# Gate blocks of the RG-LRU packed by halves of the rows, with high weights from a rounding DMA of GpSimd

## The chip, the cores and the metric

The kernel runs on one core of one Trainium2 chip. The metric is the time of one execution on the device, in microseconds, the median of several executions. One execution of each kernel is also recorded by the hardware profiler, and all views below are of that execution. The engines are named as in the profile: PE (TensorE, the matmuls; PEld are its weight loads), DVE (VectorE), ACT (ScalarE), POOL (GpSimd) and SP (SyncE, which here only issues transfers). A row of the profile such as `L127` names a line of the kernel file, which may be that of a helper.

## The reference

One decoder layer on a sequence of 512 tokens with 2048 channels, in float32. What matters here is the recurrent branch: a causal convolution of width 4, two gates by block-diagonal matrices (16 blocks of 64 channels), and a linear recurrence.

```python
h = rms_norm(x) * (1.0 + scale) + shift          # scale, shift, gate from silu(c) @ w_ada + b_ada
proj = h @ w_in                                  # xr, gr, qc, kvc, kr, ga
...
xc = causal_depthwise_conv(xr, conv_w) + conv_b
xb = xc.reshape(B, S, RNN_BLOCKS, RNN_BLOCK)     # 16 blocks of 64 channels
r = sigmoid(einsum('bshi,hij->bshj', xb, w_rg_a).reshape(B, S, C) + b_rg_a)
i = sigmoid(einsum('bshi,hij->bshj', xb, w_rg_x).reshape(B, S, C) + b_rg_x)
log_a = -LRU_C * r * softplus(-lru_lambda)
a = exp(log_a)
b = sqrt(-expm1(2.0 * log_a)) * (i * xc)
y_rnn = linear_recurrence(a, b) * silu(gr)
y_att = mla_branch(qc, kvc, kr, ...) * silu(ga)
x = x + gate * (concat(y_rnn, y_att) @ w_out)
```

## The kernel before

Everything is kept transposed: channels on the 128 rows of SBUF, the 512 tokens along a row. A float32 product is made of three matmuls in the chip's rounded float32 (`fp32r`): each operand is split into a high part, its rounded value, and a low part, the rest. `mm3` and `mm3s` issue high × high, high × low and low × high, with the weights as the stationary operand. The split of a weight tile is done by `wsplit` (L205): ACT copies the raw tile with rounding (`whi<-wraw`), and DVE subtracts (`wlo<-wraw,whi`). `wload` (L200) first issues the transfer of the raw tile on SP. The pools of these tiles hold 3 raw, 2 high and 2 low tiles (`WIDE`).

The program goes through these stages. Up to about 214 us of the profiled execution the modulation, the normalised input h and most of the input projection are computed: the input channels of w_in are taken in 16 groups of 128, and the first 9 of them are done here for all column blocks. Then comes the loop over `MORDER[:24]` (L812), to about 330 us: for each of 24 blocks of 128 output columns, `proj_last` (L528) loads a 448 KB tile (7 groups of input channels, 128 x 896 elements), issues 14 matmuls with the high weights and 7 with the low, and adds the sum to what is stored. I call one turn of this loop a step. Between the steps stand the parts of the recurrent branch for blocks of 128 channels, m = 0 to 7: `rg_conv` (L688, convolution and gates), `rg_decay`, `rg_scan` (the recurrence, one DVE instruction) and `fin_gr` (L803, product with silu(gr), and its split into yh and yl), and the latent parts of the attention (`latent`, `do_kr`). The attention stage and the output projection follow, to the end; there, generators in a list `pipe` are advanced in turn, and the remaining 8 blocks of projection and the output projection are issued as fillers between the attention's pieces.

In `rg_conv`, two blocks of 64 channels share the 128 rows. The matrix of a gate is therefore a 128 x 128 tile with two 64 x 64 blocks on its diagonal and zeros elsewhere; a tile of 128 x 256 holds both gates. The convolved input xc is split into xh and xl (ACT and DVE, 128 rows each), the weights into gh and gl, and three matmuls into bank `pr` and three into bank `pi` follow. ACT then applies the two sigmoids with their biases:

```python
mm3(pr, gh[:, 0:P], gl[:, 0:P], xh, xl, True, True)
mm3(pi, gh[:, P:2 * P], gl[:, P:2 * P], xh, xl, True, True)
tab(x, pr, AF.Sigmoid, bias=vec[:, C_BA + m:C_BA + m + 1])
tab(ig, pi, AF.Sigmoid, bias=vec[:, C_BX + m:C_BX + m + 1])
```

Two calls stand behind each of steps 4, 5, 9 and 10; `rg_decay` behind 6 and 11, the square roots behind 7 and 12. Behind steps 19 and 23 `fin_gr` is called for four blocks each.

What sets the order: each engine executes its own instructions in the order in which the program holds them, and waits there for the results that it needs. SP's order is that of the code (it is scheduled by hand). The order on PE, DVE, ACT and POOL is laid out by a list scheduler when the program is built, from its own estimates of durations; `issue_after` and the chaining of table functions in `tab` bind some instructions behind others. So an instruction that is moved or shortened in the code can change the order of its neighbours.

Of the kernel before, what the change touches and what calls it, by code (L numbers as in the profile page):

```python
# [12 lines left out]
F32 = mybir.dt.float32  # L13
F32R = mybir.dt.float32r
BF16 = mybir.dt.bfloat16
I32 = mybir.dt.int32
AF = mybir.ActivationFunctionType
ALU = mybir.AluOpType
AX = mybir.AxisListType

P = 128
S = 512
# [23 lines left out]
WARM = (7, 10)  # L46
NACC = 6
GRATE = 1.1
BANKS = dict(u=(0, 1, 3), f=(2,), sc=(4, 5), tp=(6,), op=(6,), tq=(7,), oa=(2, 3, 0, 1, 7, 4, 5, 6))
QUOTA = (13, 6, 5, 6, 10)  # L50
MAGIC = 12582912.0

C_BADA, C_CW, C_CB, C_BA, C_BX, C_LAM, C_QA, C_KVA, NVEC = 0, 48, 80, 88, 96, 104, 112, 116, 120
R_QN, R_KN, R_QR, R_KR, R_IF, R_ID, R_MK, NROW = 0, 128, 256, 320, 384, 416, 544, 672

TWO_PI = 2.0 * math.pi
# [30 lines left out]
def body(ctx, nc, tc, a):  # L87
    V, G, A, PE, DMA = nc.vector, nc.gpsimd, nc.scalar, nc.tensor, nc.sync
    last_tab = [None]

    def act(out, in_, func, **kw):
        return A.activation(out=out, in_=in_, func=func, **kw)  # L92

    def tab(out, in_, func, **kw):
        if last_tab[0] is None:
            i = act(out, in_, func, **kw)
        else:
            with tc.issue_after(last_tab[0]):
                i = act(out, in_, func, **kw)
        last_tab[0] = i.ins if hasattr(i, "ins") else i  # L100
        return i
# [9 lines left out]
    def ins_of(i):  # L111
        return i.ins if hasattr(i, "ins") else i
# [6 lines left out]
    def tt(o, x, y, op):  # L119
        return V.tensor_tensor(out=o, in0=x, in1=y, op=op)  # L120

    def split(hi, lo, src):
        act(hi, src, AF.Copy)
        return tt(lo, src, hi.bitcast(F32), ALU.subtract)
# [73 lines left out]
    wlast = [None]  # L198

    def wload(src, n, after=None):  # L200
        raw = wraw()
        DMA.dma_start(out=raw[:, :n], in_=src)
        return wsplit(raw, n, after)

    def wsplit(raw, n, after=None, hi_after=None):  # L205
        hi, lo = wtile("whi", "whi"), wtile("wlo", "wlo")
        with tc.issue_after(hi_after) if hi_after is not None else nullcontext():
            act(hi[:, :n], raw[:, :n], AF.Copy)
        with tc.issue_after(after) if after is not None else nullcontext():
            wlast[0] = ins_of(tt(lo[:, :n], raw[:, :n], hi[:, :n].bitcast(F32), ALU.subtract))  # L210
        return hi, lo

    NB = 18
    vec = cst.tile([P, NVEC], F32, name="vec")
    row = cst.tile([P, NROW], F32, name="row")
# [312 lines left out]
    def proj_last(n, kind, parts):  # L528
        ps = bank(kind, "pp")
        m = MORDER[n]  # L530
        for k0, k1 in parts:
            wh, wl = wload(a["win3"][n, :, k0 * P:k1 * P], (k1 - k0) * P)
            mm3s(ps, wh, wl, hs(KM + k0, KM + k1), k0 == 0, KM + k1 == NK)
            if KM + k1 == NK:
                if n < N1:
                    stt(slot[m], ps, b0[:, n:n + 1], slot[m], ALU.add, ALU.add)
                else:
                    tt(slot[m], ps, slot[m], ALU.add)
            yield
# [145 lines left out]
    def tmp(name):  # L685
        return rg.tile([P, S], F32, tag="t", name=name, bufs=4)

    def rg_conv(m):  # L688
        w = lambda t: vec[:, C_CW + 8 * t + m:C_CW + 8 * t + m + 1]
        x = slot[XR + m]  # L690
        xc = half(XC, xcn, xcc, "xc")
        act(xc, x, AF.Identity, scale=w(3), bias=vec[:, C_CB + m:C_CB + m + 1])
        for s in (1, 2, 3):
            stt(xc[:, s:S], x[:, 0:S - s], w(3 - s), xc[:, s:S], ALU.mult, ALU.add)
        xs = rg.tile([P, 2, S], F32R, tag="xs", name="xs", bufs=2)
        xh, xl = xs[:, 0], xs[:, 1]
        split(xh, xl, xc)
        raw = rg.tile([P, 256], F32, tag="graw", name="graw", bufs=2)
        DMA.dma_start(out=raw, in_=a["wrg"][m])
        gh = rg.tile([P, 256], F32R, tag="gh", name="gh", bufs=2)  # L700
        gl = rg.tile([P, 256], F32R, tag="gl", name="gl", bufs=2)
        split(gh, gl, raw)
        pr = bank("aux", "pr")
        mm3(pr, gh[:, 0:P], gl[:, 0:P], xh, xl, True, True)
        pi = bank("aux", "pi")
        mm3(pi, gh[:, P:2 * P], gl[:, P:2 * P], xh, xl, True, True)
        tab(x, pr, AF.Sigmoid, bias=vec[:, C_BA + m:C_BA + m + 1])
        ig = tmp("ig")
        tab(ig, pi, AF.Sigmoid, bias=vec[:, C_BX + m:C_BX + m + 1])
        tt(xc, ig, xc, ALU.mult)  # L710
        return xc

# [87 lines left out]

    yh, yl = {}, {}

    def fin_gr(m):  # L803
        yt = tmp("yt")
        tt(yt, slot[XR + m], slot[GR + m], ALU.mult)
        yh[m] = pjt(XR + m, F32R, f"yh{m}")
        yl[m] = pjt(GR + m, F32R, f"yl{m}")
        split(yh[m], yl[m], yt)

    banks(mm=(0, 1, 2, 3), aux=(4, 5, 6, 7))  # L810
    xcs, als = {}, {}
    for n, m in enumerate(MORDER[:24]):  # L812
        run(proj_last(n, "mm", ((0, 7),)))
        if n == 16:
            proj_kr(2)
            do_kr()
        if n in (19, 23):
            for m in range(n - 19, n - 15):
                tab(slot[GR + m], slot[GR + m], AF.Silu)
            for m in range(n - 19, n - 15):  # L820
                fin_gr(m)
        if n in (4, 5):
            for t in (2 * n - 8, 2 * n - 7):
                xcs[t] = rg_conv(t)
        if n == 6:
            for t in range(4):
                als[t] = rg_decay(t)
        if n in (7, 12):
            for t in range(4):
                t += 4 * (n > 7)  # L830
                tab(slot[XR + t], slot[XR + t], AF.Sqrt)
        for n0, t0 in ((7, 0), (15, 4)):
            if n0 <= n < n0 + 4:
                t = t0 + n - n0
                with tc.issue_after(wlast[0]):
                    rg_scan(t, xcs[t], als[t])
        if n in (9, 10):
            for t in (2 * n - 14, 2 * n - 13):
                xcs[t] = rg_conv(t)
        if n == 11:  # L840
            for t in range(4, 8):
                als[t] = rg_decay(t)
        if KVC <= m < KVC + 4:
            latent(m, KVC, 0, kvh, kvl, C_KVA)
        if QC <= m < QC + 4:
            latent(m, QC, 1, qh, ql, C_QA)
# [5 lines left out]
    p3ctx = ExitStack()  # L852
    p3 = p3ctx.enter_context(tc.tile_pool(name="p3", bufs=1))
    mask = p3.tile([P, S], F32, name="mask")
    V.memset(mask[:, :S - P], 0.0)
    act(mask[:, S - P:], row[:, R_MK:], AF.Copy)
    HT = FREE[5:]
    banks(**BANKS)
    KT, QT = HT[0:3], HT[3:6]
# [256 lines left out]
    def paced():  # L1116
        st = 0
        for n, _ in enumerate(fillers()):
            if n >= GSTART:
                gates(int(st * GRATE))  # L1120
                st += 1
            if n in XSTEPS:
                oload()
            yield
# [97 lines left out]
    wh, wl = wload(a["wlast"], 4 * P)  # L1222
# [21 lines left out]
def _layout(x, c, positions, w_ada, b_ada, w_in, conv_w, conv_b, w_rg_a, b_rg_a, w_rg_x, b_rg_x, lru_lambda,  # L1244
            q_a_norm, w_uq, kv_a_norm, w_ukv, q_norm_nope, q_norm_rope, k_norm_nope, k_norm_rope, w_out):
    f = np.float32
# [9 lines left out]
    cols = np.concatenate([w[:, 0:2048], w[:, 2048:2560], w[:, 2560:3072], w[:, 3136:4160]], axis=1)  # L1256
# [18 lines left out]
    kr4 = w[:, 3072:3136].reshape(NK, P, 64)  # L1275
    for ci, (k0, kc) in enumerate(KRS):
        d[f"wkr{ci}"] = con(kr4[k0:k0 + kc].transpose(1, 0, 2)).reshape(P, kc * 64)
    g = np.zeros((8, P, 2, P), f)
    for m in range(8):
        for gi, wr in enumerate((w_rg_a[0], w_rg_x[0])):  # L1280
            for b in range(2):
                g[m, b * 64:(b + 1) * 64, gi, b * 64:(b + 1) * 64] = wr[2 * m + b]
    d["wrg"] = g.reshape(8, P, 256)
    kv = w_ukv[0].reshape(4, P, 4, 2, 2, P)
    d["wkv"] = con(kv.transpose(2, 1, 0, 4, 3, 5)).reshape(4, P, 2048)
# [5 lines left out]
    v = np.zeros((P, NVEC), f)  # L1291
    v[:, 0:48] = b_ada[0].reshape(48, P).T
    v[:, C_CW:C_CW + 32] = conv_w[0].reshape(4, 8, P).transpose(2, 0, 1).reshape(P, 32)
    for col, arr in ((C_CB, conv_b), (C_BA, b_rg_a), (C_BX, b_rg_x), (C_LAM, lru_lambda)):
        v[:, col:col + 8] = arr[0].reshape(8, P).T
    for col, arr in ((C_QA, q_a_norm), (C_KVA, kv_a_norm)):
        v[:, col:col + 4] = arr[0].reshape(4, P).T
    d["vec"] = v
# [22 lines left out]
```

## Time and profile before

| | before |
|---|---|
| median of 3 executions | 703.68 us (703.63 to 703.79) |
| profiled execution, its own time | 703.65 us |
| profiled execution, span from the first to the last instruction | 701.8 us |
| granted clock of TensorE, mean | 1.000 |
| HBM read, written | 132.01 MB, 4.19 MB |

The page lists busy times of each engine and the costliest groups of instructions; further views give the waits, the chain of work that ended last, and busy times by window. A matmul's "mean ns" is the time from its start to its end; neighbouring matmuls overlap. The busy time of the engines in 40 slices of 17.5 us each, in tenths, shows that PE is busy from end to end, and where the others have room:

```profile
PE   9999999999999999999999999999999999999997
PEld 5887878888888888888888888888888888788886
DVE  6559998889996989898656667669797886673322
ACT  4664326333454689875465587787767333222220
POOL 1000000000000000011012011002120000000000
PEclk9999999999999999999999999999999999999999
DMA  9978998849954322322353335233463986874320
```

The touched loop lies in the thirteenth to the nineteenth of these slices.

### The profile page before, as it was taken

The numbers are of one execution on the slowest core, as the hardware profiler recorded it, in microseconds if no ns is written. First come the engines' busy times: TensorE is split into PE (matmuls) and PEld (weight loads), VectorE is DVE, ScalarE is ACT, GpSimd is POOL, SyncE is SP. The second block draws the span as 40 slices with busy tenths as digits, with TensorE's granted clock in tenths as the row PEclk, the third lists the DMA queues.
The fourth block names the chain that finished last, engine by engine and source line by source line (L and its number), as shares of the span: only waits on it lengthen the run. The fifth ranks groups of instructions, "written<-read, shape, count | busy, mean of one in ns | idle before, by whom it ended". The sixth has DMA issues, their size and how long they took to land.

```text
span 701.8 us, 9602 instructions
## 1 busy us (share of the span) xinstructions
PE 694.9 (99%) x3225; PEld 574.7 (82%) x3225; DVE 522.3 (74%) x1012; ACT 376.6 (54%) x812; POOL 36.5 (5%) x54
## 2 busy tenths in 40 slices
PE   9999999999999999999999999999999999999997
PEld 5887878888888888888888888888888888788886
DVE  6559998889996989898656667669797886673322
ACT  4664326333454689875465587787767333222220
POOL 1000000000000000011012011002120000000000
PEclk9999999999999999999999999999999999999999
DMA  9978998849954322322353335233463986874320
GB/s 336 405 316 326 376 404 278 309 170 385 330 203 137 115 72 79 92 80 78 117 162 100 95 119 191 84 114 111 141 209 100 302 274 246 301 251 166 105 91 30
DMA packets 52473, 136.83 MB, mean 195 GB/s; under 512 B 6085, under 2 KB 12997, under 8 KB 48457
## 3 DMA queue, kind: packets, MB, share of 16 engines
q1 hardware_dynamic: 45360, 115.25, 47.1%
q10 hardware_dynamic: 7064, 20.98, 9.0%
q8 instruction: 25, 0.41, 0.2%
q14 instruction: 24, 0.19, 0.1%
HBM read 132.01 MB, written 4.19 MB: 194 GB/s over the span
## 4 chain that ended last, share of the span: by engine, by line
PE 96%; DVE 2%; issue 1%; ACT 0%; SPq 0%; POOL 0%; DVEq 0%; POOLq 0%
PE pp L127 48%; PE oa L127 25%; PE uwkv L127 6%; PE uwq L127 5%; PE sc L127 4%; PE op L127 2%; PE tp L1015 1%; PE pk L127 1%; DVE ada L279 1%; PE tq L927 1%; PE pr L127 1%; PE pi L127 1%; PE junk_ps L127 0%; DVE wlo L120 0%; DVE h L104 0%
## 5 line engine op out<-in xcount | busy, mean ns | idle before, releaser
L92 ACT ACTIVATE whi<-wraw 128x512 fp32r<-128x512 f32 (+4 forms) x214 | 142.3, 670 | 173.6 <-PE oa L127 67.5
L127 PE MATMUL pp<-h,whi 128*128 128x512 f32 x880 | 216.2, 390 | 1.3 <-DVE h L104 1.3
L120 DVE TENSOR_TENSOR wlo<-wraw,whi 128x512 fp32r<-128x512 f32 (+4 forms) x214 | 155.9, 734 | 81.3 <-ACT whi L92 38.8
L127 PEld LDWEIGHTS pp<-h,whi 128*128 128x128 f32 x880 | 164.7, 188 | 35.8 <-DVE h L104 1.7
L127 PE MATMUL pp<-h,wlo 128*128 128x512 f32 x440 | 115.5, 391 | 0.2 <-DVE wlo L120 0.2
L127 PE MATMUL oa<-yl,whi 128*128 128x512 f32 (+1 forms) x260 | 100.9, 389 | 0.0
L127 PE MATMUL oa<-yh,whi 128*128 128x512 f32 (+1 forms) x260 | 100.1, 390 | 0.1
L127 PEld LDWEIGHTS pp<-h,wlo 128*128 128x128 f32 x440 | 82.1, 188 | 17.1 <-DVE wlo L120 0.6
L279 DVE CUSTOM_DVE_ANT_0 ada<-ada,cb,vec 128x2048 f32<-128x2048 f32 x31 | 72.7, 2345 | 1.7 <-DMA ada<-in_ada 1.7
L127 PE MATMUL oa<-yh,wlo 128*128 128x512 f32 (+1 forms) x260 | 70.9, 389 | 0.0
L127 PEld LDWEIGHTS oa<-yh,whi 128*128 128x128 f32 x260 | 48.7, 188 | 10.1 <-ACT yh L92 0.5
L127 PEld LDWEIGHTS oa<-yl,whi 128*128 128x128 f32 x260 | 48.9, 188 | 9.3
L127 PEld LDWEIGHTS oa<-yh,wlo 128*128 128x128 f32 x260 | 47.8, 188 | 9.4
L92 ACT ACTIVATE pj<-pp 128x512 f32<-128x512 f32 x50 | 29.3, 597 | 18.0 <-PE pp L127 17.4
L127 PE MATMUL pp<-e,whi 128*128 128x512 f32 x136 | 34.4, 393 | 0.0
L127 PEld LDWEIGHTS pp<-e,whi 128*128 128x128 f32 x136 | 25.5, 188 | 5.7 <-issue 0.5
L127 PE MATMUL uwkv<-whi,kvt 128*128 128x512 f32 x80 | 28.4, 397 | 0.0
L239 POOL TENSOR_TENSOR hs<-hs,mhalf 128x4 f32<-128x4 f32 (+1 forms) x20 | 25.1, 1257 | 1.6
L127 PE MATMUL uwq<-whi,kvt 128*128 128x384 f32 x80 | 24.0, 342 | 0.1
L92 ACT ACTIVATE PT<-tp 128x128 f32<-128x128 f32 (+3 forms) x32 | 14.1, 439 | 18.3 <-PE tp L1015 10.9
L127 PE MATMUL sc<-kT,qT 128*128 128x128 f32 (+3 forms) x96 | 22.9, 326 | 0.0
L92 ACT ACTIVATE yh<-yt 128x512 fp32r<-128x512 f32 x16 | 10.1, 632 | 22.2 <-DVE yt L120 22.1
(214 smaller groups left out, 964.6 us busy)
## 6 DMA issues: line engine op xcount, KB each, us to landing
ada<-in_ada SPq DMA_DIRECT2D x31, 1024.0 KB, 7.5
ada<-in_ada ACTq DMA_DIRECT2D x32, 512.0 KB, 5.3
wraw<-in_wout SPq DMA_DIRECT2D x59, 256.0 KB, 2.9
wraw<-in_win SPq DMA_DIRECT2D x24, 448.0 KB, 3.3
wraw<-in_wkv SPq DMA_DIRECT2D x24, 256.0 KB, 2.8
wraw<-in_winc SPq DMA_DIRECT2D x18, 320.0 KB, 5.2
wraw<-in_winsb SPq DMA_DIRECT2D x18, 256.0 KB, 6.9
w0t<-in_w0t SPq DMA_DIRECT2D x9, 512.0 KB, 6.8
```

Source lines behind the costliest of these rows:

```text
L92: return A.activation(out=out, in_=in_, func=func, **kw)
L120: return V.tensor_tensor(out=o, in0=x, in1=y, op=op)
L127: return PE.matmul(out=out, lhsT=lhsT, rhs=rhs, start=start, stop=stop, **kw)
L239: G.tensor_tensor(out=out, in0=out, in1=mhalf[:, :n], op=ALU.pow)
L279: ttr_last[0] = V.tensor_tensor_reduce(out=t, in0=t, in1=cv, op0=ALU.mult, op1=ALU.add, scale=1.0, scalar=vec[:, C_BADA + j:C_BADA + j + 1 ...
L927: PE.transpose(tp[:, d * 256 + i2 * P:d * 256 + (i2 + 1) * P], kt[:, q * P:(q + 1) * P], ident)
L1015: PE.transpose(tp[:, j * P:(j + 1) * P], pr[:, j * P:(j + 1) * P], ident)
```

## The change

Five things are changed.

1. *The gate blocks are packed.* For each of the two blocks of 64 channels of m (b = 0, 1), the 128 rows of the moving tile `xs[:, b]` hold the block's high part on its own 64 rows and its low part on the other 64. The stationary tile holds, on both halves of the rows, the block's weights of both gates side by side (64 columns each). One matmul with gh then gives high × high plus high × low for both gates, one with gl low × high plus low × low. The results of a block lie in one bank `pg`, one gate on each half of the rows; they are read by four sigmoids of 64 rows, where `HP` names the rows (own, other). The bias of the second gate is kept once more with its halves exchanged (`C_BXS`).
2. *The high weights of the loop's 24 steps and of the gate blocks* are no longer rounded by ACT from the raw tile; a transfer issued by POOL reads them from HBM again and rounds on the way (`wcast`, and `G.dma_start(out=gh, ...)`). The raw tile is still loaded, for the low part. The high tiles of the steps alternate between the old pool and a new one, `hi2`, with two more.
3. *`rg_conv` is called one block at a time*, behind steps 2, 3, 4, 5, 8, 9, 10 and 11 (`RGC`); the second `rg_decay` and square roots move behind 12 and 13.
4. *`fin_gr` for m = 6 and 7, and the attention's mask,* move into a generator at the start of the attention stage, with the mask's zeros set by POOL in place of DVE.
5. *The banks of the attention's first product* are taken in the order 1, 3, 0 in place of 0, 1, 3.

```diff
-BANKS = dict(u=(0, 1, 3), f=(2,), sc=(4, 5), tp=(6,), op=(6,), tq=(7,), oa=(2, 3, 0, 1, 7, 4, 5, 6))
+BANKS = dict(u=(1, 3, 0), f=(2,), sc=(4, 5), tp=(6,), op=(6,), tq=(7,), oa=(2, 3, 0, 1, 7, 4, 5, 6))
...
+    hi2 = [None, 0]
+
+    def wcast(src, n):
+        raw = wraw()
+        DMA.dma_start(out=raw[:, :n], in_=src)
+        hi2[1] += 1
+        hi = wtile("whi", "whi") if hi2[1] % 2 else hi2[0].tile([P, 2 * S], F32R, tag="whi", name="whi", bufs=2)
+        lo = wtile("wlo", "wlo")
+        G.dma_start(out=hi[:, :n], in_=src)
+        wlast[0] = ins_of(tt(lo[:, :n], raw[:, :n], hi[:, :n].bitcast(F32), ALU.subtract))
+        return hi, lo
...
-            wh, wl = wload(a["win3"][n, :, k0 * P:k1 * P], (k1 - k0) * P)
+            wh, wl = (wcast if kind == "mm" else wload)(a["win3"][n, :, k0 * P:k1 * P], (k1 - k0) * P)
...
+    hi2[0] = rgctx.enter_context(tc.tile_pool(name="hi2", bufs=1))
...
+    HP = [(slice(0, 64), slice(64, P)), (slice(64, P), slice(0, 64))]
...
-        xh, xl = xs[:, 0], xs[:, 1]
-        split(xh, xl, xc)
+        for b, (own, oth) in enumerate(HP):
+            act(xs[own, b], xc[own], AF.Copy)
+            tt(xs[oth, b], xc[own], xs[own, b].bitcast(F32), ALU.subtract)
...
-        split(gh, gl, raw)
-        pr = bank("aux", "pr")
-        mm3(pr, gh[:, 0:P], gl[:, 0:P], xh, xl, True, True)
-        pi = bank("aux", "pi")
-        mm3(pi, gh[:, P:2 * P], gl[:, P:2 * P], xh, xl, True, True)
-        tab(x, pr, AF.Sigmoid, bias=vec[:, C_BA + m:C_BA + m + 1])
+        G.dma_start(out=gh, in_=a["wrg"][m])
+        tt(gl, raw, gh.bitcast(F32), ALU.subtract)
+        pg = [bank("aux", "pg") for _ in range(2)]
+        for b in range(2):
+            mm(pg[b], gh[:, cols(b)], xs[:, b], True, False)
+            mm(pg[b], gl[:, cols(b)], xs[:, b], False, True)
         ig = tmp("ig")
-        tab(ig, pi, AF.Sigmoid, bias=vec[:, C_BX + m:C_BX + m + 1])
+        for b, (own, oth) in enumerate(HP):
+            tab(x[own], pg[b][own], AF.Sigmoid, bias=vec[own, C_BA + m:C_BA + m + 1])
+            tab(ig[own], pg[b][oth], AF.Sigmoid, bias=vec[oth, C_BXS + m:C_BXS + m + 1])
...
+    LATE = 6
+    RGC = (2, 3, 4, 5, 8, 9, 10, 11)
...
-            for m in range(n - 19, n - 15):
+            for m in range(n - 19, min(n - 15, LATE)):
                 fin_gr(m)
-        if n in (4, 5):
-            for t in (2 * n - 8, 2 * n - 7):
-                xcs[t] = rg_conv(t)
+        if n in RGC:
+            t = RGC.index(n)
+            xcs[t] = rg_conv(t)
...
-    V.memset(mask[:, :S - P], 0.0)
-    act(mask[:, S - P:], row[:, R_MK:], AF.Copy)
...
+    def late_fins():
+        yield
+        G.memset(mask[:, :S - P], 0.0)
+        act(mask[:, S - P:], row[:, R_MK:], AF.Copy)
+        for m in range(LATE, 8):
+            fin_gr(m, p3.tile([P, S], F32, tag="yt", name="yt"))
+            yield
+
+    pipe.append(late_fins())
```

What this does to the order of the instructions is shown at three places.

On PE, where the first gate block stands between the projection's matmuls (pp), `xs` being the split input and gh, gl the split gate weights. Before:

```order
L127 MATMUL pp<-h_1845,wlo 128x512
L127 MATMUL pr<-xs,gh 128x512 x2
L127 MATMUL pr<-xs,gl 128x512
L127 MATMUL pi<-xs,gh 128x512 x2
L127 MATMUL pi<-xs,gl 128x512
```

and now:

```order
L127 MATMUL pp<-h_1189,wlo 128x512
L127 MATMUL pg<-xs,gh 128x512
L127 MATMUL pg<-xs,gl 128x512
L127 MATMUL pp<-h_1283,wlo 128x512
L127 MATMUL pg<-xs,gh 128x512
L127 MATMUL pg<-xs,gl 128x512
L127 MATMUL pp<-h_1497,wlo 128x512
```

Six matmuls have become four, in two pairs with one matmul of the projection between them.

On POOL, from the last of its memsets at the program's start. Before, the first work behind it is the small arithmetic of the latent norms (rl), far into the loop:

```order
L245 MEMSET sel 128x512
L238 ISA
L238 TENSOR_SCALAR rl<-ls_2593 128x4
L239 TENSOR_TENSOR rl<-rl,mhalf 128x4
L238 TENSOR_SCALAR rl<-ls_2747 128x4
```

and now, with the numbers of the tiles (whi the high weights of one step, gh those of one gate block):

```order
L257 MEMSET sel_106 128x512
L221 DMA whi_1993<-in_win3 128x896
L718 DMA gh_2060<-in_wrg 128x256
L221 DMA whi_2079<-in_win3 128x896
L718 DMA gh_2116<-in_wrg 128x256
L221 DMA whi_1964<-in_win3 128x896
L221 DMA whi_2022<-in_win3 128x896
L221 DMA whi_2135<-in_win3 128x896
```

POOL now issues 32 transfers, in this order, and the rl arithmetic stands behind the nineteenth transfer of step weights. The first transfer waits until the tiles whose place the pool `hi2` takes are given up by the stage before; whi_1964, whi_2022 and whi_2135 wait for the buffers of the old pool, the last of them for PE's last matmul with whi_1964 and DVE's subtraction from it.

On PE at the start of the loop, with the numbers of the tiles: pp_1927 is the last piece of the stage before, wlo_1930 its low weights. Before:

```order
L127 MATMUL pp_1927<-h8_945,whi_1929 128x512 x2
L127 MATMUL pp_1927<-h4_637,wlo_1930 128x512
L127 MATMUL pp_1927<-h5_729,wlo_1930 128x512
L127 MATMUL pp_1927<-h6_813,wlo_1930 128x512
L127 MATMUL pp_1927<-h7_861,wlo_1930 128x512
L127 MATMUL pp_1927<-h8_945,wlo_1930 128x512
L127 MATMUL pp_1958<-h9_1037,whi_1961 128x512 x2
```

and now:

```order
L127 MATMUL pp_1927<-h8_945,whi_1929 128x512 x2
L127 MATMUL pp_2076<-h9_1037,whi_2079 128x512 x2
L127 MATMUL pp_2076<-h10_1189,whi_2079 128x512 x2
L127 MATMUL pp_2076<-h11_1283,whi_2079 128x512 x2
L127 MATMUL pp_2076<-h12_1497,whi_2079 128x512 x2
L127 MATMUL pp_1927<-h4_637,wlo_1930 128x512
L127 MATMUL pp_1927<-h5_729,wlo_1930 128x512
```

The high matmuls of one later step (whi_2079) have moved ahead of the rest. Behind them PE goes through 14 matmuls with whi_1964 and 7 with its low weights, then 14 and 7 with whi_1993, 14 and 7 with whi_2022, and then to whi_2135, which takes the buffer of whi_1964.

More of the change, by code (lines that the diff above doesn't have):

```diff
@@ L48 @@
 GRATE = 1.1
-BANKS = dict(u=(0, 1, 3), f=(2,), sc=(4, 5), tp=(6,), op=(6,), tq=(7,), oa=(2, 3, 0, 1, 7, 4, 5, 6))
+BANKS = dict(u=(1, 3, 0), f=(2,), sc=(4, 5), tp=(6,), op=(6,), tq=(7,), oa=(2, 3, 0, 1, 7, 4, 5, 6))
 QUOTA = (13, 6, 5, 6, 10)
 MAGIC = 12582912.0
-C_BADA, C_CW, C_CB, C_BA, C_BX, C_LAM, C_QA, C_KVA, NVEC = 0, 48, 80, 88, 96, 104, 112, 116, 120
+C_BADA, C_CW, C_CB, C_BA, C_BX, C_LAM, C_QA, C_KVA, C_BXS, NVEC = 0, 48, 80, 88, 96, 104, 112, 116, 120, 128
 R_QN, R_KN, R_QR, R_KR, R_IF, R_ID, R_MK, NROW = 0, 128, 256, 320, 384, 416, 544, 672
@@ L801, in body, with fin_gr @@
     yh, yl = {}, {}
-    def fin_gr(m):
-        yt = tmp("yt")
+    def fin_gr(m, yt=None):
+        yt = tmp("yt") if yt is None else yt
         tt(yt, slot[XR + m], slot[GR + m], ALU.mult)
@@ L827, in body @@
                 als[t] = rg_decay(t)
-        if n in (7, 12):
+        if n in (7, 13):
             for t in range(4):
@@ L836, in body @@
                     rg_scan(t, xcs[t], als[t])
[L837 to L840, printed above, removed]
+        if n == 12:
             for t in range(4, 8):
@@ L1277, in _layout @@
         d[f"wkr{ci}"] = con(kr4[k0:k0 + kc].transpose(1, 0, 2)).reshape(P, kc * 64)
-    g = np.zeros((8, P, 2, P), f)
+    g = np.zeros((8, 2, 64, 2, 2, 64), f)
     for m in range(8):
-        for gi, wr in enumerate((w_rg_a[0], w_rg_x[0])):
-            for b in range(2):
-                g[m, b * 64:(b + 1) * 64, gi, b * 64:(b + 1) * 64] = wr[2 * m + b]
+        for b in range(2):
+            for gi, wr in enumerate((w_rg_a[0], w_rg_x[0])):
+                g[m, :, :, b, gi ^ b] = wr[2 * m + b]
     d["wrg"] = g.reshape(8, P, 256)
@@ L1295, in _layout @@
         v[:, col:col + 8] = arr[0].reshape(8, P).T
+    v[:, C_BXS:C_BXS + 8] = np.roll(v[:, C_BX:C_BX + 8], 64, axis=0)
     for col, arr in ((C_QA, q_a_norm), (C_KVA, kv_a_norm)):
```

## The prediction

> **What bounds the kernel now.** I read four views in this order: the busy times, the stage that the change touches, the list of what TensorE waited for, and the chain of work that ended last.
>
> ```profile
> span 701.8 us, 9602 instructions
> ...
> PE 694.9 (99%) x3225; PEld 574.7 (82%) x3225; DVE 522.3 (74%) x1012; ACT 376.6 (54%) x812; POOL 36.5 (5%) x54
> ...
> 214.00:330.00 116.00, 116.00 (x525) 96.33 (x524) 99.62 (x148) 85.27 (x128) 5.00 (x6) 1.00 0.31 95
> ```
>
> The last row is the window of the touched stage (columns: length, busy time and count of PE, of weight loads, of DVE, ACT and POOL, granted clock, DMA share, GB/s). The k-tail projections and the gate blocks run in it, PE is busy in all of its 116 us at a clock of 1.00, DVE in 86% (99.62 of 116), ACT in 74%, and the transfers fill 0.31 of the DMA engines.
>
> A busy PE could still hide waits, so I read next what PE waited for in the whole span (total, times, longest):
>
> ```profile
> PE pp L127 <- DVE h L104: 1.3, 1, 1.3
> PE junk_ps L127 <- POOL junk L230: 1.0, 1, 1.0
> PE pp L127 <- DVE xs L116: 0.6, 1, 0.6
> PE pp L127 <- DVE wlo L120: 0.2, 1, 0.2
> ```
>
> These are 3.1 us, and none lies in the stage: the chain of work there has PE pieces alone, end to end.
>
> ```profile
> by line: PE pp L127 85.9%; PE pr L127 4.7%; PE pi L127 4.7%; PE pk L127 2.7%; PE lps L127 1.4%; PE krt L771 0.4%; PE ktp L797 0.4%
> ...
> 213.89 24.25 PE pp L127 x107
> 238.14 0.68 PE pr L127 x3
> 238.82 0.68 PE pi L127 x3
> ```
>
> So 107 projection matmuls take 24.25 us, 0.2266 us each, and three gate matmuls take 0.68, again 0.2267 each. The time of this kernel is the number of matmuls times that pitch; no other engine is waited for. A change gains here only by fewer matmuls, and loses only where it makes PE wait.
>
> **The matmuls removed.** A gate block has 6 matmuls of 512 columns before (three for pr, three for pi) and 4 after, as the order in front of this shows; 8 blocks make 48 and 32. The chain gives pr and pi 9.4% of 116 us, 10.9 us, which is 48 × 0.2267 = 10.88. Sixteen fewer are 16 × 0.2267 = **3.63 us**, all on the path.
>
> The groups give another price for the same instruction:
>
> ```profile
> L127 PE MATMUL pi<-xs,gh 128*128 128x512 f32 x16 | 5.6, 389 | 0.0
> ```
>
> 389 ns is the length of one matmul from start to end, and by it the gain would be 6.2 us. But neighbours overlap: the pieces of the chain, with their counts, say how long PE is held for one, and I go by them.
>
> **What ACT and DVE get and lose.** These are the rows for the edits (mean ns behind the bar's comma):
>
> ```profile
> L92 ACT ACTIVATE whi<-wraw 128x896 fp32r<-128x896 f32 x24 | 22.7, 948 | 8.6 <-PE pp L127 6.9 <-issue 1.6
> L92 ACT ACTIVATE gh<-graw 128x256 fp32r<-128x256 f32 x8 | 3.2, 410 | 1.7 <-DMA graw<-in_wrg 1.7
> L92 ACT ACTIVATE xs<-xc 128x512 fp32r<-128x512 f32 x8 | 5.0, 629 | 3.9 <-DVE xc L104 3.9
> L92 ACT ACTIVATE ig<-pi,vec 128x512 f32<-128x512 f32 x8 | 5.5, 687 | 0.0
> L92 ACT ACTIVATE qp<-tqe 64x512 fp32r<-64x512 f32 x8 | 4.7, 590 | 0.6 <-PE tqe L975 0.5
> L120 DVE TENSOR_TENSOR qp<-tqe,qp 64x512 fp32r<-64x512 f32 x8 | 5.5, 688 | 2.6 <-ACT qp L92 2.4
> L120 DVE TENSOR_TENSOR xs<-xc,xs 128x512 fp32r<-128x512 f32 x8 | 5.5, 682 | 0.9 <-ACT xs L92 0.9
> L120 DVE TENSOR_TENSOR yl<-yt,yh 128x512 fp32r<-128x512 f32 x16 | 10.8, 688 | 3.7 <-ACT yh L92 3.6
> ```
>
> The qp rows show that 64 rows cost what 128 do (688 ns against the 682 of xs). So a block's two half splits cost DVE 2 × 0.69 in place of 0.68, and its four half sigmoids cost ACT 4 × 0.69 in place of two. ACT loses 22.7 + 3.2 us and gains 8 × (0.63 + 2 × 0.69) = 16.1, so about 10 us fewer. DVE gains 8 × 0.69 = 5.5 us and gives up the product and the split of gated outputs 6 and 7, 2 × 2 × 0.69 = 2.7 by the row of yl, to the attention stage: net +2.8, 102.4 of 112.4 us, 91%. On the path both count nothing, since PE waits for neither engine in this stage; the cover is the one to two steps by which the low weights are ahead. If it is gone, at most the 2.8 us reappear. The moved work of outputs 6 and 7 and of the mask lands where PE has 100% too (33.00 of 33.00), with DVE and ACT half free:
>
> ```profile
> 347.00:380.00 33.00, 33.00 (x160) 28.42 (x159) 20.25 (x46) 18.49 (x57) 5.04 (x6) 1.00 0.47 146
> ```
>
> I price it at nothing. The mask goes to POOL; a memset there of 128x512 takes 527 ns before:
>
> ```profile
> L245 POOL MEMSET sel<- 128x512 f32 x1 | 0.5, 527 | 0.0
> L238 POOL TENSOR_SCALAR hs<-hs 128x4 f32<-128x4 f32 x16 | 3.3, 209 | 161.8 <-DVE hs L120 128.4 <-PE pp L127 33.2
> ```
>
> Queued behind it are the hs rows of the query and key norms, which have 161.8 / 16 = 10 us of idle time each: nothing. The first attention unit takes banks 1 and 3 in place of 0 and 1. Its weight load waits now for the store of the last projection:
>
> ```profile
> 346.28 0.30 PEld L127 LDWEIGHTS uwq<-whi,kvt 128*128 128x128 f32 x2 [0.41 <-DVE pj L120]
> ```
>
> That wait may go, or another store may take its place: 0.4 us either way, and I take none.
>
> **The transfers added.** Each of 24 steps and 8 blocks reads its weights a second time, 24 × 448 KB + 8 × 128 KB, about 12.1 MB, into 112 us. What the stage moves now:
>
> ```profile
> q1 hardware_dynamic: 4320, 10.91, 31.1%
> ...
> wraw<-in_win SPq DMA_DIRECT2D x21, 448.0 KB, 3.3
> ...
> DMA to landing us min/median/max: 2.3/3.4/12.0
> 160.00:180.00 20.00, 20.00 (x90) 16.57 (x89) 20.00 (x41) 8.99 (x14) 0.00 (x0) 1.00 0.97 374
> ```
>
> At the present price (31.1% of 116 us for 10.91 MB, 3.3 us a MB) the added 12.1 MB need 40 us of the engines: the share goes from 0.31 to about 0.68. They would fill the engines only if a rounding transfer cost twice a plain one; the window 160 to 180 carries 374 GB/s with PE whole. No row shows a transfer issued by POOL, nor one that rounds. Its time to landing I bound by the rows of wraw, 2.3 to 12.0 us (all sizes), and take the 3.3 of the same tile from the other queue. The lead: in the order of after, between the last use of whi_1964 and the first of whi_2135, which reuses its buffer, stand 7 + 14 + 7 + 14 + 7 = 49 matmuls, **11.1 us**. So 3.3 is hidden with 7.8 us to spare, and at 12.0 the step would wait 0.9.
>
> [...]
>
> POOL's own time per issue no row shows either. The nearest are SP's 0.33 us for an issue and POOL's arithmetic, 1.02; I take 1.0, and from 0.3 to 2.0 the 32 issues fill 10 to 64 us of an engine that is busy 5 of 116. At the stage's start POOL's first transfer waits until the tiles of the stage before are given up:
>
> ```profile
> 314.81 0.33 SPq L202 DMA_DIRECT2D wraw<-in_win  x1
> 305.39 1.02 POOL L239 TENSOR_TENSOR rl<-rl,mhalf 128x4 f32<-128x4 f32 x1
> ...
> 202.47 0.08 DVE L279 DVE_READ_ACCUMULATOR2_ANT mod<- 128x1 f32 x1
> ...
> 213.04 1.30 PE L127 MATMUL pp<-h,wlo 128*128 128x512 f32 x5
> ```
>
> The first rounded weights on PE are those of whi_2079, at the place that 213.04 has now. From 202.55 that is 10.5 us, less two issues of 1.0 ahead of it, 8.5 against 3.3: hidden.
>
> **The sum.** 701.8 us of span plus 1.85 us around it is the profiled execution's 703.65, at the median of 703.68. 703.65 − 3.63 = **700.0**. Below that little is to be had, since PE waits for nothing in the stage: I allow 0.5 for the banks.
>
> **Rivals.** *POOL is held by DVE, and the rounded weights come late (slower).* This speaks for it:
>
> ```profile
> 305.12 0.20 POOL L238 TENSOR_SCALAR rl<-ls 128x4 f32<-128x4 f32 x1 [302.80 <-DVE ls L743]
> ...
> 313.87 1.57 POOL L238 TENSOR_SCALAR rl<-ls 128x4 f32<-128x4 f32 x1 [7.46 <-DVE ls L743]
> ...
> 313.70 1.08 DVE L120 TENSOR_TENSOR wlo<-wraw,whi 128x896 fp32r<-128x896 f32 x1
> 314.70 0.68 DVE L120 TENSOR_TENSOR xc<-pj,xc 128x512 f32<-128x512 f32 x1
> ...
> 258.00:270.00 12.00, 12.00 (x55) 9.94 (x54) 11.82 (x18) 11.95 (x20) 0.00 (x0) 1.00 0.26 78
> 270.00:278.00 8.00, 8.00 (x37) 6.64 (x36) 8.00 (x11) 7.99 (x14) 0.00 (x0) 1.00 0.14 51
> ```
>
> The same small POOL instruction took 0.20 us once and 1.57 once, and the long one ended at 315.44, when DVE's two subtractions had ended (315.38). If issuing a transfer is held alike, it passes only in DVE's pauses. From 258 to 278 DVE has 0.2 us of them. It decides from a hold of 7.8 us on, the lead less the landing; a hold of the whole 20 us costs 20 − 7.8 = 12.2, so 700.0 + 12.2 = **712.2**. [...] Chance 0.12, in which I count a rounding transfer of over twice the plain price.
>
> [...]
>
> *DVE falls behind.* At 91% in the stage, and near 100% in the rows above already, the added half splits could delay the low weights. Priced at up to the net 2.8 us, so at most **702.8**, evenly from 700 on. For it: the packed rows; against it: PE waits for no low weight in those same rows now. Chance 0.10.
>
> *The first steps wait.* If the first landings take the 12.0 us of wraw's longest, step one lacks 12.0 − 8.5 = 3.5: **703.5**. For it: the traffic before 200 us; against it: the stage's share of 0.31. Chance 0.05.
>
> That the matmuls aren't saved is no rival, as the order shows their count.
>
> **Chances.** The forecast, 700.0, has 0.73. Faster by over 0.2% (1.4 us, about what a measurement of this kernel tells from no change), so under 702.3: the forecast and half of DVE's case, 0.78; within 0.2%: 0.10; slower: 0.12. The range goes from 699.5, the allowance, to 702.8, the end of DVE's case, and leaves out 0.17.
>
> **What would show it.** Right: pg x4 pieces of 0.91 us a block and no wait of PE on whi, wlo or gh between 200 and 345 us; the stage some 3.6 us shorter, the rest unmoved; POOL's transfers landing within 8 us. Wrong: PE waiting for a DMA of whi, POOL rows that end with DVE's, a DMA share near 1.0, or PE waiting for DVE's wlo in the stage.

## The result, and the profile after

| | before | after |
|---|---|---|
| median | 703.68 us (703.60 to 704.27, 5 runs) | 700.69 us (700.18 to 700.99, 5 runs) |
| ratio after / before | | 0.9954, 95% interval 0.9939 to 0.9969 |
| profiled execution, its own time | 703.65 us | 700.74 us |

The kernel became 3.0 us faster, 2.9 in the profiled executions. The page of after, with the rows of the new transfers (a queue's row has packets, MB and share of the 16 DMA engines; a transfer's row ends with the median us to landing):

```profile
span 698.9 us, 9638 instructions
...
PE 691.8 (99%) x3209; PEld 570.8 (82%) x3209; DVE 526.9 (75%) x1019; ACT 370.5 (53%) x804; POOL 52.4 (7%) x87
...
q0 software_dynamic: 4608, 12.06, 6.1%
...
L221 POOL DMA_DIRECT2D whi<-in_win x24 | 13.1, 547 | 276.0 <-DMA wraw<-in_win 201.0
...
wraw<-in_win SPq DMA_DIRECT2D x24, 448.0 KB, 4.0
whi<-in_win POOLq DMA_DIRECT2D x24, 448.0 KB, 3.9
```

PE executes 3209 matmuls, 16 fewer than before. The rounding transfers are the queue q0, 12.06 MB; one lands 3.9 us after its issue, and POOL spends 0.55 us on it.

The stage of the change and its most crowded stretch, by windows of after (length, busy time and count of PE, weight loads, DVE, ACT, POOL, granted clock, DMA share, GB/s):

```profile
214.00:330.00 116.00, 115.87 (x521) 95.07 (x520) 103.69 (x152) 81.58 (x121) 17.82 (x33) 1.00 0.61 186
258.00:278.00 20.00, 20.00 (x90) 16.56 (x89) 19.78 (x30) 19.77 (x30) 3.19 (x6) 1.00 0.67 199
```

PE is as full as before, the transfers have gone from 0.31 to 0.61 of the engines, and from 258 to 278 us DVE and ACT have 0.2 us of pause each in 20, as in before (0.2 and 0.1).

Where the time went is seen by the first matmul of the attention stage, `uwq`, in the timeline of PE (start, length). In before it stands here:

```profile
345.34 0.51 PE L127 MATMUL uwq<-whi,kvt 128*128 128x384 f32 x2
```

and in after here:

```profile
342.69 0.87 PE L127 MATMUL uwq<-whi,kvt 128*128 128x384 f32 x4
```

So 2.65 of the 2.9 us lie ahead of the attention stage. Sixteen matmuls at the pitch of 0.2267 are 3.63: about 1.0 us of the gain is missing in the loop. The list of what PE's matmuls waited for is empty there (200 to 400 us); that of its weight loads is not (total, times, longest):

```profile
PEld pg L127 <- ACT ig L92: 0.7, 2, 0.4
PEld krt L789 <- DVE pj L120: 0.5, 1, 0.5
PEld lps L127 <- DVE lacc L120: 0.4, 1, 0.4
PEld uwq L127 <- ACT whi L92: 0.3, 1, 0.3
```

These four waits are 1.9 us; the matmuls behind the weight loads were held for a part of that. From the starts of neighbouring pieces and the pitch, PE's gaps of over 0.04 us between 250 us and the first `uwq` add up to 1.3 us in after and 0.45 in before: 0.9 more, which is nearly all that is missing.

### The profile page after: what moved, and what is told of

It is laid out like the page before. It is cut to its first block, busy times and chain, and to the rows that moved or that the text cites. A ratio compares the mean times of both kernels' runs of the same rounds, so it can differ in the third digit from the quotient of the medians.

```text
span 698.9 us, 9638 instructions
## 1 busy us (share of the span) xinstructions
PE 691.8 (99%) x3209; PEld 570.8 (82%) x3209; DVE 526.9 (75%) x1019; ACT 370.5 (53%) x804; POOL 52.4 (7%) x87
## 3 DMA queue, kind: packets, MB, share of 16 engines
q0 software_dynamic: 4608, 12.06, 6.1%
## 4 chain that ended last, share of the span: by engine, by line
PE 72%; DVE 7%; ACT 3%; issue 2%; DMA 0%; POOL 0%; DVEq 0%; POOLq 0%; ACTq 0%
PE pp L127 26%; PE oa L127 25%; PE uwkv L127 6%; PE uwq L127 5%; PE sc L127 4%; PE op L127 2%; DVE xc L104 1%; PE tp L1030 1%; DVE wlo L120 1%; DVE pj L104 1%; DVE pj L744 1%; PE tq L942 1%; DVE xc L120 1%; ACT pj L92 1%; DVE xs L120 1%
## 5 line engine op out<-in xcount | busy, mean ns | idle before, releaser
L92 ACT ACTIVATE whi<-wraw 128x512 fp32r<-128x512 f32 (+3 forms) x190 | 119.5, 634 | 169.1 <-PE oa L127 59.9
L221 POOL DMA_DIRECT2D whi<-in_win x24 | 13.1, 547 | 276.0 <-DMA wraw<-in_win 201.0
L127 PE MATMUL uwkv<-whi,kvt 128*128 128x512 f32 x80 | 28.4, 397 | 0.0
L92 ACT ACTIVATE yh<-yt 128x512 fp32r<-128x512 f32 x16 | 10.1, 632 | 24.4 <-DVE yt L120 24.3
```

The source lines that it names most:

```text
L127: return PE.matmul(out=out, lhsT=lhsT, rhs=rhs, start=start, stop=stop, **kw)
L221: G.dma_start(out=hi[:, :n], in_=src)
```

## The experiments

Each kernel was timed in five rounds beside the kernel before on the same chip.

### Only the transfers, without the packing

The kernel before, with the high weights of the steps and of the gate blocks from rounding transfers and four high tiles; six matmuls a block, as before.

```diff
-            wh, wl = wload(a["win3"][n, :, k0 * P:k1 * P], (k1 - k0) * P)
+            wh, wl = (wcast if kind == "mm" else wload)(a["win3"][n, :, k0 * P:k1 * P], (k1 - k0) * P)
...
-        split(gh, gl, raw)
+        G.dma_start(out=gh, in_=a["wrg"][m])
+        tt(gl, raw, gh.bitcast(F32), ALU.subtract)
```

> The kernel before with the rounding transfers of GpSimd alone (step weights and gate weights), gate blocks not packed, 48 gate matmuls. Theory A: 703.7 us, no change within 0.5, although ACT is about 26 us less busy. Rival B: 701 to 702.5 us. Rival C, these transfers cost PE something that the packing hides: above 704.4 us.

Measured: 703.53 us (703.46 to 704.42), ratio 0.9999, 0.999 to 1.0008. ACT's busy time in 214 to 330 us fell from 85.27 to 64.89 us, and the time did not move:

```profile
214.00:330.00 116.00, 115.94 (x524) 95.99 (x523) 99.96 (x148) 64.89 (x99) 18.98 (x33) 1.00 0.62 186
```

Relieving ACT and adding 12 MB of reads are worth nothing by themselves; what after gains comes with the matmuls.

### Packed, but ACT rounds

```diff
-        G.dma_start(out=hi[:, :n], in_=src)
+        act(hi[:, :n], raw[:, :n], AF.Copy)
...
-        G.dma_start(out=gh, in_=a["wrg"][m])
+        act(gh, raw, AF.Copy)
```

> Packed gate blocks as in the changed kernel, but ACT rounds the high weights again (the transfers of GpSimd are gone, the four buffers stay). Theory A, the time goes with the number of matmuls (16 fewer at 0.2267 us): 700.2 to 701.2 us, the same as the changed kernel, ACT in the loop about 26 us busier and PE waiting under 2 us for it. Rival B, the gain needs ACT's relief by the rounding transfers: 702.5 us or more, PE waiting for ACT's whi.

Measured: 707.70 us (706.77 to 708.04), ratio 1.0055, 1.0042 to 1.0068: the packing alone is slower than the kernel before, and 7.0 us slower than after. By its time this is Rival B, but PE waits for ACT's sigmoids (ig), not for whi. The list of what PE waited for, 200 to 400 us:

```profile
PE pg L127 <- ACT ig L92: 2.3, 1, 2.3
PE krt L789 <- DVE pj L120: 0.9, 1, 0.9
PE lps L127 <- DVE lacc L120: 0.4, 1, 0.4
```

A gate block waits for its bank, which the sigmoids of an earlier block have not yet read, since ACT is behind (98.90 of 116 us busy in the stage, against 85.27 in before). But the waits are 3.6 us, and the profiled execution is 6.0 longer than that of after (706.77 against 700.74). The windows behind the 2.3 us, which end at 282.82, show part of the rest:

```profile
284.00:285.00 1.00, 1.00 (x4) 0.68 (x3) 1.00 (x3) 0.96 (x3) 0.00 (x0) 0.56 0.00 0
285.00:286.00 1.00, 1.00 (x4) 0.81 (x3) 1.00 (x2) 0.97 (x2) 0.00 (x0) 0.50 0.00 0
286.00:287.00 1.00, 1.00 (x4) 0.71 (x3) 1.00 (x3) 0.96 (x2) 0.00 (x0) 0.50 0.00 0
287.00:288.00 1.00, 1.00 (x5) 0.83 (x4) 1.00 (x2) 1.00 (x2) 0.00 (x0) 0.73 0.00 0
```

PE is busy in each, but the granted clock is 0.50: over these four rows 0.44 + 0.50 + 0.50 + 0.27 = 1.7 us are lost with PE at work. This pause cost more than its 2.3 us.

### All of fin_gr back in the loop, and more of it out

```diff
-    LATE = 6
+    LATE = 8
```

> The changed kernel, but the gated outputs 6 and 7 are split in the loop as before (only the mask stays moved): DVE has 2.8 us more in the loop. If DVE's cover in the loop is one to two steps (theory A): within 0.5 us of the changed kernel, 700.2 to 701.2. If DVE is at its edge there (rival D): 702 to 703.5 us, with PE waiting for DVE at the end of the loop.

Measured: 706.19 us (705.15 to 707.14), ratio 1.0034, 1.0022 to 1.0047; 5.5 us slower than after for two products and two splits of DVE, and more than either theory allowed. The timeline of PE (in brackets the idle time before the piece and its releaser):

```profile
345.02 0.34 PE L127 MATMUL uwq<-whi,kvt 128*128 128x384 f32 x1
348.37 0.98 PE L127 MATMUL uwq<-wlo,kvt 128*128 128x384 f32 x2 [3.01 <-DVE wlo L120]
```

and the windows from there on:

```profile
345.00:348.00 3.00, 0.36 (x3) 0.04 (x1) 2.23 (x4) 0.88 (x3) 0.00 (x0) 0.88 0.01 5
348.00:350.00 2.00, 1.63 (x5) 1.66 (x6) 2.00 (x5) 1.70 (x4) 0.00 (x0) 0.50 0.29 69
350.00:352.00 2.00, 2.00 (x7) 2.00 (x7) 1.44 (x3) 0.74 (x2) 0.42 (x1) 0.50 0.83 249
...
354.00:356.00 2.00, 2.00 (x10) 1.65 (x9) 0.00 (x0) 0.10 (x1) 0.00 (x0) 0.97 0.59 208
```

One wait of 3.0 us, then 5.7 us at half the clock, or 2.9 us lost: together 5.9 of the 6.4 us between this profiled execution (707.14) and that of after. What stands ahead of the low weights of `uwq` in DVE's timeline is the product and the split that were put back, and DVE waits there for ACT:

```profile
345.07 0.69 DVE L120 TENSOR_TENSOR yt<-pj,pj 128x512 f32<-128x512 f32 x1 [2.50 <-ACT pj L92]
346.46 0.69 DVE L120 TENSOR_TENSOR yl<-yt,yh 128x512 fp32r<-128x512 f32 x1 [0.70 <-ACT yh L92]
347.07 0.68 DVE L120 TENSOR_TENSOR pj<-pp,pj 128x512 f32<-128x512 f32 x1
347.67 1.49 DVE L120 TENSOR_TENSOR wlo<-wraw,whi 128x384 fp32r<-128x384 f32 x3
```

So the move of outputs 6 and 7 is not a free rearrangement: it is less DVE's 2.7 us of work that it takes away than two of DVE's waits ahead of weights that PE needs at once. (ACT is late there in its turn: ahead of the instruction that DVE waits 2.50 us for, it waited 0.96 and 0.85 us for raw weights of `uwq` to land.) With `LATE = 4` two more outputs leave the loop.

> The changed kernel with the gated outputs 4 to 7 moved to the attention stage: DVE has 2.8 us less in the loop. Theory A: within 0.3 us of the changed kernel. Rival D, DVE's lag in the loop is what is missing of the 3.63 us: 0.5 to 0.7 us faster, near 700.0, and the pieces of idle PE between 300 and 345 us gone.

Measured: 700.80 us (700.29 to 701.10), ratio 0.9959, 0.9946 to 0.9971, as after; the waits at krt and lps stay at 0.5 and 0.4. They do not come from outputs 4 to 7, and Rival D falls.

### What the pause costs beside its length

The kernel with `LATE = 8`, and 14 copies of the first query matmul ahead of the point where PE waited; the same 14 in after as a control.

```diff
+                    if g == 0 and u == 0 and name == "wq" and kn == 0 and ph == 0 and i == 0:
+                        for _ in range(14):
+                            mm(o, xh[k][:, t], wh[:, :n], True, True)
                     if ph:
                         mm(o, xh[k][:, t], wl[:, :n], False, kn == 3)
```

> The kernel with outputs 6 and 7 split in the loop again, and 14 copies of the first query-up-projection matmul (384 columns) ahead of it; each starts its bank anew, so the result is the same, and TensorE has about 14 x 0.17 = 2.4 us more to do. They lie where it waited 3.0 us for the low weights. Theory C (after a pause of 2 us or more the granted clock falls to 0.50 for some 6 us, which costs about 3 us beside the pause): the wait shrinks to about 0.7 us, the clock stays at 1.00, TensorE goes on when VectorE is done as before, and the time FALLS from 706.2 to about 703.2 (702.6 to 703.8) although there is more work. Rival W (the loss of that kernel is waiting and order, the clock only a mark of it): 706.2 if all copies hide in the wait, up to 708.6 if none does.

> Control: the changed kernel with the same 14 copies. It has no pause there, so the copies come on top: 700.7 + 2.4 = 703.1 (702.6 to 703.4) by Theory C and by Rival W, the clock at 1.00. If it stays at 700.7, the copies are hidden somewhere and say nothing of the other run.

Measured: 704.62 us (703.98 to 705.14), ratio 1.0009, 1.0001 to 1.0018, for the filled kernel with `LATE = 8`, whose interval lies below that of the unfilled one; 702.61 us (702.32 to 702.87), ratio 0.9982, 0.9973 to 0.9991, for the control. The same stretch in the filled kernel, waits first, then windows:

```profile
PE uwq L127 <- DVE wlo L120: 1.0, 1, 1.0
PE uwq L127 <- ACT whi L92: 0.5, 1, 0.5
```

```profile
348.00:350.00 2.00, 1.74 (x10) 1.35 (x8) 1.30 (x4) 0.89 (x2) 0.00 (x0) 1.00 0.62 186
350.00:352.00 2.00, 1.80 (x9) 1.71 (x10) 1.53 (x3) 0.87 (x3) 0.42 (x1) 1.00 0.52 174
352.00:354.00 2.00, 2.00 (x11) 1.74 (x11) 0.00 (x0) 0.59 (x3) 0.00 (x0) 1.00 0.88 270
```

In after the copies cost 1.9 us. In the kernel with the pause they made it 1.6 us faster, though 14 matmuls were added: the clock stays at 1.00. The fall shows that the clock, not the wait alone, makes the price; Rival W falls. It stays above the 702.6 to 703.8 of Theory C, because waits of 1.0 and 0.5 us are left where 0.7 was expected, and the clock gave back less than the 3 us taken: from the end of the wait to the end of the span the unfilled kernel needs 705.4 − 348.37 = 357.0 us, the filled one 702.9 − 347.68 = 355.2 with another wait of 0.5 in it, so 2.3 us. Not all of the difference is the clock's: DVE's low weights also came 0.7 us earlier in the filled kernel (347.68 against 348.37).

### Twice the rounding traffic, and two high tiles in place of four

```diff
         G.dma_start(out=hi[:, :n], in_=src)
+        G.dma_start(out=hi[:, :n], in_=src)
```

> The changed kernel with each rounding transfer of the step weights issued twice into the same tile, the second behind the first: 11 MB more, and the weights land after about 8 us (twice 3.9) instead of 3.9. Theory A, with a lead of 11.1 us: hidden but for a few steps, 700.2 to 704 us. Rival E, the transfers are at their limit already (the loop's DMA share is 0.49 to 0.83): 708 us or more, share near 1.0.

Measured: 711.70 us (708.53 to 713.27), ratio 1.0106, 1.0087 to 1.0125. The list of what PE waited for, between 200 and 345 us, has one row:

```profile
PE pp L127 <- DMA whi<-in_win: 7.6, 5, 3.8
```

and the stage by windows:

```profile
214.00:330.00 116.00, 108.36 (x463) 87.88 (x461) 97.55 (x138) 78.64 (x117) 25.60 (x49) 0.96 0.81 252
```

With the second copy the step's weights come late, at a DMA share of 0.81; the mean clock of 0.96 is the mark of the pauses. The time is that of Rival E, but the share isn't near 1.0. POOL shows another limit: before the second copies it waits 17 times, 56.3 us in all, on the tile that the first copy fills, and issues nothing else meanwhile. With a median of 4.8 us to landing for each copy and an issue of 0.53 between them, a step's weights take an estimated 10.1 us of the lead of 11.1. So the transfers of after are hidden, but not two of them one behind the other; what as much traffic would do without that order isn't shown.

```diff
-        hi = wtile("whi", "whi") if hi2[1] % 2 else hi2[0].tile([P, 2 * S], F32R, tag="whi", name="whi", bufs=2)
+        hi = wtile("whi", "whi")
```

> The changed kernel without the pool hi2: the high weights have two buffers instead of four, so the lead from the last use of a buffer to its next first use falls from 49 matmuls (11.1 us) to 7 to 28 (1.6 to 6.3 us), against 3.9 us of landing and 0.53 of issue. Theory A: PE begins to wait for transfers, 702 to 712 us. Rival F, the lead doesn't matter since the order puts the uses far apart: 700.2 to 701.2 us.

Measured: 706.45 us (705.99 to 707.59), ratio 1.0040, 1.0026 to 1.0054. PE's waits, 200 to 345 us:

```profile
PE pk L127 <- DVE wkhl L120: 2.8, 1, 2.8
PE pg L127 <- ACT ig L92: 1.6, 1, 1.6
```

The time is in the range of Theory A, but no matmul waits for a transfer by this list; what is late is work of DVE and ACT. (Smaller waits for rounding transfers are there: one weight load waits 0.5 us for whi, and DVE 1.2 us for gh at 234 us.) The two more tiles are needed, though not for the reason that PE would meet an unlanded weight; how the delay runs from the tiles to these two waits wasn't followed.

### The calls in pairs again

```diff
-    RGC = (2, 3, 4, 5, 8, 9, 10, 11)
+    RGC = (4, 4, 5, 5, 9, 9, 10, 10)
-            t = RGC.index(n)
-            xcs[t] = rg_conv(t)
+            for t in (k for k in range(8) if RGC[k] == n):
+                xcs[t] = rg_conv(t)
```

> The changed kernel with the gate blocks called in pairs behind steps 4, 5, 9 and 10 as before, instead of one at a time. Theory A: the number of matmuls is the same, 700.2 to 701.2 us. Rival G, the spreading carries part of the gain: 701.5 to 703 us, with PE waiting for ACT's sigmoids or DVE's splits at the pairs.

Measured: 700.48 us (700.32 to 700.85), ratio 0.9954, 0.9941 to 0.9966, as after. Calling `rg_conv` one block at a time brings nothing that can be measured.

### ACT rounds where it is idle

Ten of the 24 steps, the first 4 and the last 6, are given back to ACT:

```diff
-        G.dma_start(out=hi[:, :n], in_=src)
+        if 5 <= hi2[1] <= 18:
+            G.dma_start(out=hi[:, :n], in_=src)
+        else:
+            act(hi[:, :n], raw[:, :n], AF.Copy)
```

> The changed kernel, but ScalarE rounds the high weights of the first 4 and the last 6 of the 24 steps; 14 steps and the gate blocks keep the rounding transfers. ScalarE gets 10 x 0.95 = 9.5 us more, before about 230 us and after about 300, where it is busy 14 to 40% and 35 to 85%. Theory A (the relief counts only where ScalarE is full, 234 to 304 us): 700.7 (700.3 to 701.2), no wait of TensorE over 0.5 us. Rival B (each rounding that goes back to ScalarE costs its share of the 7.0 us that all 32 cost): 700.7 + 7.0 x 10/32 = 702.9.

Measured: 699.39 us (699.29 to 699.92), ratio 0.9937, 0.9924 to 0.9949. Both theories missed: it is 1.3 us faster than after. No wait of a weight load on ACT or DVE is left between 200 and 400 us, and the attention stage begins here:

```profile
341.65 0.87 PE L127 MATMUL uwq<-whi,kvt 128*128 128x384 f32 x4
```

345.34 − 341.65 = 3.69, against the 3.63 of sixteen matmuls: the whole gain. Which of the two ends of the loop does it? The conditions for that were `if hi2[1] <= 18:` (the last 6 on ACT) and `if hi2[1] >= 5:` (the first 4).

> The changed kernel, but ScalarE rounds the high weights of the last 6 steps only (ScalarE +5.7 us, all behind about 300 us). The run before it (first 4 and last 6) took 699.39, 1.3 less than the changed kernel, and TensorE's small waits at 279, 315, 320 and 345 us were gone. Theory T (the waits come from the end of the loop: there VectorE stands idle for 3.3 us between 294 and 314 behind ScalarE and then delays TensorE; with the last 6 on ScalarE the planner orders that stretch otherwise): 699.4 (699.2 to 699.8), VectorE idle under 1 us there. Theory S (they come from the loop's start, where fewer transfers let the gate blocks begin earlier): 700.7.

> The changed kernel, but ScalarE rounds the high weights of the first 4 steps only (ScalarE +3.8 us, before about 230 us). Theory T: 700.7 (700.3 to 701.0), with VectorE's 3.3 us of idle time between 294 and 314 and TensorE's small waits still there. Theory S: 699.4.

Measured: 700.79 us (700.66 to 701.81), ratio 0.9962, 0.9950 to 0.9975, with the last 6; 699.39 us (698.95 to 700.01), ratio 0.9939, 0.9925 to 0.9953, with the first 4. Theory T falls, Theory S holds: the waits at the end have their cause at the loop's beginning. The loop's own length shows it free of shifts ahead of it. From a group of 20 matmuls that starts at 166.58 us in before to the first `uwq` it is 178.76 us in before and 176.18 in after; it is 175.02 with ten steps on ACT, 175.02 with the first 4 and 176.12 with the last 6. After gains 2.58 us there, and the two better kernels 3.74. The timeline of PE in after, at the first step's low weights and at the first and third gate block:

```profile
220.45 1.75 PE L127 MATMUL pp<-h,wlo 128*128 128x512 f32 x7
...
233.60 0.39 PE L127 MATMUL pg<-xs,gh 128*128 128x512 f32 x1
...
249.92 0.39 PE L127 MATMUL pg<-xs,gh 128*128 128x512 f32 x1
```

and the same three in the kernel with ten steps on ACT:

```profile
218.09 1.75 PE L127 MATMUL pp<-h,wlo 128*128 128x512 f32 x7
...
231.23 0.39 PE L127 MATMUL pg<-xs,gh 128*128 128x512 f32 x1
...
242.79 0.39 PE L127 MATMUL pg<-xs,gh 128*128 128x512 f32 x1
```

PE waits for nothing in either between 190 and 278 us, so the places differ by the order that the scheduler laid out: with ACT's rounding it puts the first step 2.4 us earlier, and the third gate block 7.1. That the earlier gate blocks remove the later waits is argued from these places, not shown: from 258 to 278 us DVE and ACT are as full here as in after (19.78 and 19.68 of 20). Whether transfers with another order would do the same wasn't tried.

These two kernels, the ten steps and the first 4 on ACT, are the best of the study: 4.2 to 4.3 us under before, where after has 3.0. Against after their intervals overlap, but their ten runs (up to 700.01) all lie below those of after (from 700.18).

## Why the prediction was right, and where it was not

- *Fewer matmuls at the pitch of PE* (700.0 forecast, 700.69 measured). Right in mechanism: with transfers alone nothing is gained, and where no wait is in the way the loop gains 3.7 us. After falls 0.7 us short of the term: the small pauses of PE on ACT and DVE between 278 and 346 us take about 0.9, and some of that comes back later (from the first `uwq` to the end it is 356.2 us in after and 356.5 in before). The pauses are the second rival, *DVE falls behind*, in small, and it is ACT as often as DVE.
- *ACT about 10 us fewer, DVE +2.8.* Over the span ACT fell from 376.6 to 370.5 us, 6.1. The groups give the 10, but records of neighbouring instructions overlap, and a sum of groups counts that time twice: from 200 to 345 us ACT's groups add up to 109.7 us in before and 100.1 in after, 9.6 fewer, where it was busy for 100.66 and 95.11, 5.6 fewer. That is the difference. DVE went from 99.62 to 103.69 of 116 in the stage, 89% against the 91% forecast.
- *"If it is gone, at most the 2.8 us reappear."* This is the step that failed, though it did not decide the result. Without the rounding transfers the cover is gone on ACT's side, and 7.0 us appear; with outputs 6 and 7 back in DVE's order, 5.5. The price had left out that delay gathered into one pause (3.0 us with `LATE = 8`, 2.3 where ACT rounds), and that the clock fell to 0.50 with it. "On the path both count nothing" held only for the parts together: the rounding transfers and the moved outputs, priced at nothing, are what makes the 3 us possible.
- *Transfers hidden, 3.3 us to landing in a lead of 11.1.* Right: no matmul waits for one in after. They took 3.9 us, and the share was 0.61 in the stage, not 0.68. From 200 to 330 us the two queues of after have these rows:

```profile
q0 software_dynamic: 4608, 12.06, 32.6%
q1 hardware_dynamic: 4929, 12.86, 30.5%
```

  32.6% of 130 us for 12.06 MB are 3.5 us a MB, 30.5% for 12.86 are 3.1: a MB of the rounding queue was 1.14 times as dear here, and 1.10 times in the run with twice the traffic (53.1% for 20.78 MB against 28.4% for 12.17). With each transfer issued twice the cover was gone, but at a share of 0.81: the engines weren't full, as the step had it for a price twice as high.
- *POOL's issue, 1.0 us, and the rival that DVE holds it.* It was 0.55 on average. In after, for the tile whi:

```profile
L221 POOL DMA_DIRECT2D whi<-in_win x24: 527/530/730, 203.4 to 325.0; - x24
```

  Minimum, median and maximum are 527, 530 and 730 ns, beside a DVE that is busy 19.78 of 20 us from 258 to 278. The longest is the first one, at 203 us. No issue was held as the small POOL instruction was in before, which took 1.57 us; why an issue passes where that one was long isn't shown.
- *The first steps wait* (703.5). PE didn't wait there. But the first four steps are where the last 1.3 us were to be had, by the order and not by a wait.
- *The late outputs, the mask and the banks at nothing.* Right for the place where they went; from 347 to 380 us PE in after is still busy for 33.00 of 33.00 us, with the clock at 1.00. Mask and banks weren't tried alone.

## What to carry to other kernels

Where one engine is full from end to end, removed instructions can be worth their pitch, as here 3.69 us against 3.63, provided that its feeders keep their lead. A feeder's busy share in the most crowded 20 us doesn't tell whether they do: ACT has 19.94 us there before, 19.77 in after and 19.81 where it rounds, and the same packing gains 3 us in the second and loses 4 in the third. So look in the feeder's order for what stands ahead of the work that the full engine needs next. Price a lost lead by the pause that it becomes, and for the clock add what it cost here, 1.5 to 2.9 us (half of the 3.1 to 5.7 us at 0.50), where the pause is as long as those that had a fall with them, 1.8 us and more. Relief on another path (a rounding transfer) isn't worth the same at each step: giving back the first four brought 1.3 us, the last six nothing, by the order that followed from it.

## What the runs showed of the hardware

**The clock fell with pauses of 1.8 us and more.** All pauses of PE over 0.95 us between 200 and 360 us, in the profiles of five kernels:

| kernel | idle time of PE, us | granted clock behind it |
|---|---|---|
| `LATE = 8`, filled | 1.0 | 1.00 |
| twice the traffic, at 304 us | 1.5 | 1.00 |
| two high tiles, at 275 us | 1.6 | 1.00 |
| twice the traffic, at 323 us | 1.8 | 0.50 |
| ACT rounds | 2.3 | 0.50 |
| two high tiles, at 310 us | 2.8 | 0.50 |
| `LATE = 8` | 3.0 | 0.50 |
| twice the traffic, at 237 us | 3.8 | 0.50 |

The time at 0.50 with PE at work was 3.1 us behind the 2.8, 3.4 behind the 2.3 and 5.7 behind the 3.0.

The rows of the granted clock show how long each fall lasted. A mean of 0.56 from 284 to 285 us puts the fall at 284.12, and the 0.73 from 287 to 288 the return at 287.54. In the same way the clock is at 0.50 from 347.3 to 354.1 with `LATE = 8`, from 309.3 to 312.7 with two high tiles, and from 235.2 to 242.0 and 323.9 to 327.3 with twice the traffic. Each stretch is 3.4 us or twice that. With `LATE = 8` the fall came inside the pause (345.36 to 348.37); where ACT rounds it came 1.3 us behind the pause's end (282.82). In the 3.4 us that end at each of the five falls PE was idle for 1.8 to 2.5 us, and at work for the rest. The three pauses of 1.0 to 1.6 us had no fall with them, and the five of 1.8 to 3.8 all had one. Where the limit lies between 1.6 and 1.8 us, and whether a pause's length alone decides, isn't shown, so a pause of 1.5 us isn't known to be safe.

**A rounding transfer was cheap here.** 448 KB from HBM with rounding landed in 3.9 us, beside plain ones of the same size at 4.0, and cost POOL 0.55 us; the engines' time for a MB of its queue was 1.10 to 1.14 times that of the plain one, by the two runs above.
